# A two-layer gating and pooling encoder on one core: where ScalarE's roundings and norm steps stand in its queue

## The chip, the core and the metric

The kernel runs on one core of a Trainium2 chip. Its engines run side by side, each through its own queue in order: TensorE (PE) multiplies, VectorE (DVE) adds and subtracts, ScalarE (ACT) computes functions and copies, GpSimd (POOL) does little here, and SyncE (SP) issues the transfers from and to memory. The metric is the device time of one launch in microseconds. All times are in microseconds unless ns is written.

## The reference

Two groups of rows share the weights: 1024 rows of a prompt and 32 rows of a running stream, 1024 channels each. There are two layers. Layer 0 mixes rows by spatial gating, layer 1 by trailing means over 2, 4, 8 and 16 rows. Each layer then has a feed-forward net (FFN) with 4096 hidden channels.

```
def sgu_mixer(h, w_in, g_v, w_s, b_s, w_out, T):
    z = jax.nn.gelu(h @ w_in)
    u, v = jnp.split(z, 2, axis=-1)
    v = rmsnorm(v, g_v)
    ...
    s = jnp.einsum('gij,bnjgd->bnigd', w, vr)
    ...
    return (u * s) @ w_out, v

for i in range(DEPTH):
    mod = jax.nn.silu(c) @ w_ada[i] + b_ada[i]
    sh1, sc1, gt1, sh2, sc2, gt2 = jnp.split(mod[:, None, :], N_MOD, axis=-1)
    h = rmsnorm(x, g_norm[i, 0]) * (1 + sc1) + sh1
    ...
    x = x + gt1 * rmsnorm(mix, g_norm[i, 1])
    h = rmsnorm(x, g_norm[i, 2]) * (1 + sc2) + sh2
    f = jnp.square(jax.nn.relu(h @ ffn_w_up[i])) @ ffn_w_down[i]
    x = x + gt2 * rmsnorm(f, g_norm[i, 3])
```

## The kernel before

**Numbers in two halves.** Every fp32 operand of a product is split into a rounded high half and the rest: wh and wl of a weight, hh and hl of an input, fh and fl (FFN) or ush and usl (gating) of a hidden value. A product is three matmuls, wh by high, wh by low, wl by high (`products`, L1134 to L1136). ACT makes the high half by a Copy that rounds; DVE subtracts to get the low half. So a hidden costs one ACT and one DVE step (`split`, L1453) and a 512 KB weight piece of 128x1024 costs one ACT step (`do_w`, L592) and one DVE step.

**Tiles and passes.** The rows lie in three tiles of 384, 384 and 288 columns. Gating works over groups of 256 of its 2048 channels, FFN over chunks of 512 hidden channels. In gating, `sgu_item.up` makes pu = weights by input and gelu gives u (L1600); wsT is the transpose of the group's spatial weights, DVE copies it and scales it into wr, psp = wr by v is the spatial product, s = psp times u, and po collects the down product from ush and usl. In FFN, `ffn_item` makes pf, relu, square and the split, and pg collects the down product. The results are added up in acc.

**Pairs.** Two gating passes and chunks 1 to 7 of each FFN handle the first two tiles at once in a scheme with fewer products (`pair_item`). Its products pfa, pfb and pfc take combinations of the two tiles' inputs and of weight quarters (A1, S31, S24, A22, made by `quads`: subtractions on DVE, roundings L546 and L564 on ACT). In one step `up(jp)` PE makes A1 into pfa, S31 into pfb, S24 into pfa, S24 into pfb, S31 into pfa, A1 into pfc, A22 into pfa. Between products ACT copies pfa and pfb out (a1, b1, a2, a3, `copy`, L1764) and DVE adds them to the hidden sums r12, r22 and r11. The last product A22 goes into pfa and so needs a3 to be out. Each r gets relu, square (L1742, L1743) and a split.

**Weights' stream.** All weight pieces and the conditioning weights form one list. `issue` starts a piece's transfer on SP when one of three raw slots is free. `stream_step` rounds the next piece; `need_w` takes steps until a weight is there, and `weave`, called between products, takes a step or two ahead of need. `weave` also draws steps of the norms and residuals (generators in `fillers`), each of which yields a number of microseconds until its next step. The program keeps an account of PE's and DVE's time while it writes the instructions; `landed` is the account's time at issue plus LANDING, 5 us. `stream_waits` holds a step back while the piece has not landed in the account, but only if `last_copy` is set and the piece is not among the next two needed.

**Order.** A scheduler orders each engine's queue. `behind_copy()` puts an ACT step behind the step in `last_copy`. In the kernel before that is the newest `copy` of an FFN pair chunk; it is unset elsewhere: in gating, in the single FFN chunks, in the third tile's chunks, and after a pair chunk's second `up`. The roundings at L546, L564 and L592 all stand in `behind_copy()`.

**Norms.** `Stat.square` gathers squares; `split_sum` (L958) splits their sum into two halves (sc by an Identity on ACT, sm on DVE); `finish` waits, multiplies the halves by ones (pn, L1005) and takes Abs_reciprocal_sqrt and Square on ACT (L1009, L1010). The names end in rs, r_0x or r_1x by norm and tile.

Of the kernel before, what the change touches and what calls it, by code (L numbers as in the profile page):

```python
# [11 lines left out]
AF = mybir.ActivationFunctionType  # L12
# [4 lines left out]
D = 1024  # L17
# [18 lines left out]
def tile_stream_encoder_step(  # L36
# [26 lines left out]
    act = nc.scalar.activation  # L63
# [6 lines left out]
    def tick(us):  # L70
        time["pe"] += us
        time["dve"] = max(time["dve"], time["pe"] - 4.0)
# [33 lines left out]
    def acc_tile(t):  # L106
# [19 lines left out]
        out=quad, in_=ident.rearrange("p (c m) -> p m c", m=32), op=ALU.add, axis=AX.X  # L126
# [4 lines left out]
    epsT = const.tile([P, 1], F32, name="eps")  # L131
# [12 lines left out]
    def ps_up(name):  # L144
        return psum.tile([P, 512], F32, tag="pu", bufs=2, name=name)

    def ps_dn(name):
        return psum.tile([P, 512], F32, tag="pd", bufs=3, name=name)

    def ps_ms(name):  # L150
        return psum.tile([P, 512], F32, tag="pm", bufs=3, name=name)

    def t_m(name):
        return work.tile([P, 384], F32, tag="m", bufs=3, name=name)

    def t_c(name):
        return work.tile([P, 384], F32, tag="c", bufs=3, name=name)

    def t_hid(kind, name, dtype=F32R):
        return work.tile([P, 384], dtype, tag="h" + kind, bufs=5, name=name)  # L160
# [321 lines left out]
    last_copy = [None]  # L482

    def behind_copy():
        return ExitStack() if last_copy[0] is None else tc.issue_after(last_copy[0])
# [341 lines left out]
    def need_w(key):  # L827
        state["used"] = max(state["used"], wpos[key])
        while key not in witem:
            assert stream_ready(), key  # L830
            stream_step()
        return witem[key]
# [8 lines left out]
    def w_finish(key):  # L841
        w_free(key)
# [35 lines left out]
    def weave(streams=1):  # L878
        if streams:
            n = 0  # L880
            run_deferred()
            while n < streams and stream_ready() and not stream_waits():
                turn = bool(subs) and stream[state["next"]][0] == "wide"
                stream_step()
                n += not turn
        while time["dve"] < time["pe"] - slack[0] and fillers:
            if not pull():
                break

    def finish(tag):  # L890
        while any(f[0] == tag for f in fillers):
            pull(True)
        time["pe"] = max(time["pe"], time["dve"] - 3.0)
# [26 lines left out]
    class Stat:  # L920
# [4 lines left out]
        def __init__(self, t, tag, split=True, small=False):  # L925
            self.t, self.tag, self.n, self.split, self.small = t, tag, ncol[t], split, small
            self.todo = []
# [27 lines left out]

        def split_sum(self, sq):
            a, b = (x[:, : self.n] for x in self.parts)
            act(out=a, in_=sq, func=AF.Identity, bias=epsT)  # L958
            stt(out=b, in0=sq, scalar=epsT, in1=a.bitcast(F32), op0=ALU.add, op1=ALU.subtract)

        def square(self, k, src=None):
# [37 lines left out]

        def finish(self, out):  # L1000
            n = self.n
            yield 3.0 if gating_now[0] else 1.2
            pn = ps_ms(f"pn_{self.tag}")
            for i, x in enumerate(self.parts):
                mm(pn[:, :n], onesr, x[:, :n], start=i == 0, stop=i == 1)  # L1005
            tick(0.4)
            q = t_m(f"q_{self.tag}")[:, :n]
            r = work.tile([P, 384], F32, tag="rr", bufs=2, name=f"r_{self.tag}")[:, :n]
            act(out=r, in_=pn[:, :n], func=AF.Abs_reciprocal_sqrt, scale=1.0 / D)  # L1009
            act(out=q, in_=r, func=AF.Square)  # L1010
            yield 2.5
            stt(out=q, in0=pn[:, :n], scalar=-0.5 / D, in1=q, op0=ALU.mult, op1=ALU.mult)
            stt(out=r, in0=q, scalar=1.5, in1=r, op0=ALU.add, op1=ALU.mult)
            out.append(r)
            yield False


    gating_now = [True]
# [110 lines left out]
    def products(ps, n, terms, of=None):  # L1129

        i0, last = (0, len(terms) - 1) if of is None else (of[0], of[1] - 1)
        tick(3 * len(terms) * (0.004 + n / 2265.0))
        for i, (wh, wl, rh, rl) in enumerate(terms, i0):
            mm(ps[:, :n], wh, rh, start=i == 0, stop=False)  # L1134
            mm(ps[:, :n], wh, rl, start=False, stop=False)  # L1135
            mm(ps[:, :n], wl, rh, start=False, stop=i == last)  # L1136
# [100 lines left out]
    with tc.manual_schedule():  # L1237
# [63 lines left out]
        ps = ps_ms("pv0_5")  # L1301
# [105 lines left out]
    for p, b in v_order:  # L1407
        ps = ps_dn(f"pv{p}_{b}")
# [40 lines left out]
    def flush():  # L1449
        while pending:  # L1450
            pending.pop(0)()

    def split(dst_hi, dst_lo, src, n):  # L1453
        act(out=dst_hi[:, :n], in_=src[:, :n], func=AF.Copy)  # L1454
        tt(out=dst_lo[:, :n], in0=src[:, :n], in1=dst_hi[:, :n].bitcast(F32), op=ALU.subtract)

    def accumulate(t, d, ps, first):
        n = ncol[t]
        if first:
            act(out=A(t, d), in_=ps[:, :n], func=AF.Copy)  # L1460
        else:
            tt(out=A(t, d), in0=A(t, d), in1=ps[:, :n], op=ALU.add)

    def up_terms(wkey, t):
        wh, wl = need_w(wkey)
        return [
            (wh[:, k * P : (k + 1) * P], wl[:, k * P : (k + 1) * P], hh[t][:, k, :], hl[t][:, k, :])
            for k in range(KB)
        ]
# [106 lines left out]
    def sgu_item(p, t, mix, after):  # L1576
        gs, tiles = mixes[p]
        last = t == tiles[-1]
        n = ncol[t]
        hid = []  # L1580

        def put(g, k, s):
            a, b = t_hid("h", f"ush{g}_{t}_{k}"), t_hid("l", f"usl{g}_{t}_{k}")
            split(a, b, s, n)
            hid.append((a, b))

        inputs, factors, spatial, gate = gating(t, mix, put)
        us = []

        def up(g, k):  # L1590
            if k == 0:
                inputs(g)
            ps = ps_up(f"pu{g}_{t}_{k}")
            products(ps, n, up_terms(("u", p, g, k), t))
            if k == 0:
                factors(g)
            if last:
                w_finish(("u", p, g, k))
            u = t_m(f"u{g}_{t}_{k}")
            act(out=u[:, :n], in_=ps[:, :n], func=AF.Gelu_apprx_tanh)  # L1600
            us.append(u)

        def down():
            for d in range(KB):
                ps = ps_dn(f"po{gs[0]}_{t}_{d}")
                terms = []
                for j, (a, b) in enumerate(hid):
                    wh, wl = need_w(("o", p, gs[j // 2], d // 4))
                    o = (j % 2) * 512 + (d % 4) * P
                    terms.append((wh[:, o : o + P], wl[:, o : o + P], a[:, :n], b[:, :n]))  # L1610
                products(ps, n, terms)
                accumulate(t, d, ps, gs[0] == (4 if t == 0 else 0))
                if d == 0 and after is not None:
                    st = Stat(t, f"rs_{t}")
                if after is not None:
                    st.square(d)
                if last and d % 4 == 3:
                    for g in gs:
                        w_finish(("o", p, g, d // 4))
                weave(d % 2)  # L1620
            if after is not None:
                after(st)

        for j in range(4):
            up(gs[j // 2], j % 2)
            if j % 2 == 1:
                gate(gs[j // 2], spatial(gs[j // 2]), us)
            weave(2 if len(tiles) == 1 else 1)
            if j == 0:
                flush()  # L1630
        pending.append(down)
# [80 lines left out]
    def pair_item(p, after, ends, gate=None):  # L1712
        l, c, tiles, _ = passes[p] if gate is None else ("u", p[1], PAIR, 1)
        n = ncol[0]
# [47 lines left out]
        def copy(ps, name):  # L1762
            x = t_c(name)
            i = act(out=x, in_=ps[:, :n], func=AF.Copy)  # L1764
            if gate is None:
                last_copy[0] = i.ins
            return x

        def add(a, b, name):
# [4 lines left out]
        def up(jp):  # L1774
# [10 lines left out]
            if jp == 0:  # L1785
                flush()
                finish("combos" if gate is None else "usums")
                if state["kept"]:
                    state["kept"] = 0
                    for i in range(2):  # L1790
                        x = w_tile(f"fu{i}", ("fu", i))
                        u_places.append((x[:, :n], x[:, n : 2 * n]))
            quad_product(pb, jp, ("S31", 512), 1, True)
            b1 = copy(pb, f"b1{name}")
            hook(2, jp)
            weave()
# [61 lines left out]
        if passes[p + 1][2] != PAIR:  # L1858
            slack[0] = 0.0
            finish(f"ffn{l}_{NT - 1}")  # L1860
            fillers.append(late_norm.pop())
# [521 lines left out]
```

## Time and profile before

| what | value |
|---|---|
| median of 3 runs | 2099.66 us (2099.4 to 2100.45) |
| profiled execution | 2097.82 us, span 2096.0 us |
| granted TensorE clock | 0.999 |
| memory read and written | 271.09 MB and 30.66 MB |
| ACT busy, DVE busy | 51%, 78% of the span |

A row of a stretch gives the busy time of each engine in it. A row of the timeline gives start, duration, engine, line, operation, output and inputs, and in brackets the idle time ahead of it and what ended that. The end of a matmul is modelled: consecutive matmuls overlap in the drawing. L80 is the line of the DVE helper, so DVE's steps are told apart by their tiles.

### The profile page before, as it was taken

The page shows a single profiled execution, that of the slowest core. Times are in us where ns is not written, and L with a number is a line of the kernel's source. Part 1 is how long each engine was busy: PE and PEld are TensorE (multiplying, and loading weights), DVE is VectorE, ACT ScalarE, POOL GpSimd, SP SyncE. Part 2 cuts the span into 40 slices and gives each one's busy share as a digit, 9 for nine tenths or more (in the row PEclk, how much of TensorE's full clock was granted, in tenths as well). Part 3 has the DMA queues.
Part 4 walks back from the last instruction along what each step waited for, and adds up shares of the span by engine and source line. Part 5 has one row for each costly group of instructions (what it writes and reads, how often), then busy time and mean ns, then how long its engine had stood idle before and what let it go on. Part 6 is the DMA issues. An engine that isn't in the chain of part 4 may idle for free.

```text
span 2096.0 us, 32878 instructions
## 1 busy us (share of the span) xinstructions
PE 2075.2 (99%) x12742; PEld 2004.8 (96%) x12742; DVE 1636.7 (78%) x2953; ACT 1060.3 (51%) x1902; POOL 22.3 (1%) x44
## 2 busy tenths in 40 slices
PE   8999999999999999999999999999999999999998
PEld 6878999999999999999999999999999999999998
DVE  6799786889789998888868989896867654569554
ACT  5633443454247643344446766675435443365555
POOL 0000000000000000000000000000000000001100
PEclk9999999999999999999999999999999999999999
DMA  8585534365444443343424667643223221148863
GB/s 296 164 264 181 185 109 131 116 208 181 139 128 138 131 136 111 121 131 111 131 83 141 206 195 240 192 142 98 91 76 113 84 81 59 53 125 230 204 178 93
DMA packets 410737, 303.91 MB, mean 145 GB/s; under 512 B 47022, under 2 KB 373974, under 8 KB 410580
## 3 DMA queue, kind: packets, MB, share of 16 engines
q1 hardware_dynamic: 409652, 300.52, 47.4%
q8 instruction: 100, 1.64, 0.3%
q0 software_dynamic: 896, 1.28, 0.2%
q14 instruction: 57, 0.47, 0.1%
q10 hardware_dynamic: 32, 0.01, 0.0%
HBM read 271.09 MB, written 30.66 MB: 144 GB/s over the span
## 4 chain that ended last, share of the span: by engine, by line
PE 88%; DVE 7%; DMA 2%; ACT 2%; issue 1%; SPq 0%; DVEq 0%; ACTq 0%
PE pg L1135 11%; PE pg L1134 11%; PE pg L1136 11%; PE pf L1134 4%; PE pf L1136 4%; PE pf L1135 4%; PE pfa L1758 3%; PE pfa L1760 3%; PE pfa L1759 3%; PE pv L1160 2%; PE pv L1162 2%; PE pv L1161 2%; PE po L1134 2%; PE po L1135 2%; PE po L1136 2%; PE pu L1134 2%
## 5 line engine op out<-in xcount | busy, mean ns | idle before, releaser
L1134 PE MATMUL pg<-fh,wh_dn 128*128 128x384 f32 (+1 forms) x960 | 311.4, 325 | 1.4 <-ACT fh L1454 1.0
L1135 PE MATMUL pg<-fl,wh_dn 128*128 128x384 f32 (+1 forms) x960 | 310.4, 323 | 0.1
L1136 PE MATMUL pg<-fh,wl_dn 128*128 128x384 f32 (+1 forms) x960 | 309.9, 323 | 0.0
L80 DVE TENSOR_TENSOR acc<-acc,pg 128x384 f32<-128x384 f32 (+1 forms) x272 | 143.8, 533 | 106.0 <-PE pg L1136 105.4
L80 DVE TENSOR_TENSOR wl_dn<-raw,wh_dn 128x1024 fp32r<-128x1024 f32 x136 | 166.0, 1221 | 71.2 <-ACT wh_dn L592 43.0
L80 DVE SCALAR_TENSOR_TENSOR aa<-raw,csil,aa 128x512 f32<-128x512 f32 (+1 forms) x364 | 208.4, 619 | 6.3 <-DMA raw<-in_w_ada_dram 5.8
L1134 PE MATMUL pf<-hh,wh_up 128*128 128x288 f32 (+1 forms) x632 | 192.3, 305 | 0.0
L1135 PE MATMUL pf<-hl,wh_up 128*128 128x288 f32 (+1 forms) x632 | 191.1, 302 | 0.0
L1136 PE MATMUL pf<-hh,wl_up 128*128 128x288 f32 (+1 forms) x632 | 190.8, 302 | 0.0
L1134 PEld LDWEIGHTS pg<-fh,wh_dn 128*128 128x128 f32 x960 | 180.1, 188 | 3.0 <-ACT fh L1454 1.6
L592 ACT ACTIVATE wh_dn<-raw 128x1024 fp32r<-128x1024 f32 x136 | 143.7, 1057 | 75.2 <-PE pf L1135 34.0
L1135 PEld LDWEIGHTS pg<-fl,wh_dn 128*128 128x128 f32 x960 | 180.2, 188 | 1.0 <-DVE fl L80 0.6
L1136 PEld LDWEIGHTS pg<-fh,wl_dn 128*128 128x128 f32 x960 | 180.2, 188 | 0.0
L592 ACT ACTIVATE wh_up<-raw 128x1024 fp32r<-128x1024 f32 x79 | 83.6, 1058 | 79.0 <-PE pg L1135 46.0
L1136 PEld LDWEIGHTS pf<-hh,wl_up 128*128 128x128 f32 x632 | 118.9, 188 | 0.3 <-DVE wl_up L80 0.3
L1135 PEld LDWEIGHTS pf<-hl,wh_up 128*128 128x128 f32 x632 | 118.6, 188 | 0.5
L1134 PEld LDWEIGHTS pf<-hh,wh_up 128*128 128x128 f32 x632 | 118.5, 187 | 0.6 <-ACT wh_up L592 0.2
L80 DVE TENSOR_TENSOR wl_up<-raw,wh_up 128x1024 fp32r<-128x1024 f32 x79 | 96.4, 1220 | 28.7 <-ACT wh_up L592 28.7
L1134 PE MATMUL pg<-fx,wh_dn 128*128 128x288 f32 (+1 forms) x352 | 109.4, 311 | 0.2 <-ACT fx L1454 0.2
L1764 ACT ACTIVATE a<-pfa 128x384 f32<-128x384 f32 x84 | 40.9, 487 | 133.6 <-PE pfa L1760 133.5
L1135 PE MATMUL pg<-fx,wh_dn 128*128 128x288 f32 (+1 forms) x352 | 108.3, 308 | 0.0
L1136 PE MATMUL pg<-fx,wl_dn 128*128 128x288 f32 (+1 forms) x352 | 108.0, 307 | 0.0
(825 smaller groups left out, 5675.4 us busy)
## 6 DMA issues: line engine op xcount, KB each, us to landing
raw<-in_ffn_w_up_dram SPq DMA_DIRECT2D x136, 512.0 KB, 4.0
raw<-in_ffn_w_down_dram SPq DMA_DIRECT2D x136, 512.0 KB, 4.1
raw<-in_w_ada_dram SPq DMA_DIRECT2D x90, 512.0 KB, 4.2
raw<-in_sgu_w_in_dram SPq DMA_DIRECT2D x48, 512.0 KB, 4.4
raw<-in_sgu_w_out_dram SPq DMA_DIRECT2D x32, 512.0 KB, 3.6
xd<-acc SPq DMA_DIRECT2D x8, 1536.0 KB, 8.4
xo_r<-xd SPq DMA_DIRECT2D x32, 384.0 KB, 4.5
vd<-vt SPq DMA_DIRECT2D x32, 256.0 KB, 3.8
```

Of the source, the lines that this page charges most:

```text
L80: return op(out, *args, **kw)
L592: act(out=wh, in_=r, func=AF.Copy)
L1134: mm(ps[:, :n], wh, rh, start=i == 0, stop=False)
L1135: mm(ps[:, :n], wh, rl, start=False, stop=False)
L1136: mm(ps[:, :n], wl, rh, start=False, stop=i == last)
L1160: mm(ps[:m, :], a_h, wh[:, o : o + 512], start=k == 0, stop=False)
L1161: mm(ps[:m, :], a_h, wl[:, o : o + 512], start=False, stop=False)
L1162: mm(ps[:m, :], a_l, wh[:, o : o + 512], start=False, stop=k == KB - 1)
L1758: mm(ps[:, :n], wh[:, o], rh, start=first and k == 0, stop=False, skip_group_check=True)
L1759: mm(ps[:, :n], wh[:, o], rl, start=False, stop=False, skip_group_check=True)
L1760: mm(ps[:, :n], wl[:, o], rh, start=False, stop=k == HK - 1, skip_group_check=True)
L1764: i = act(out=x, in_=ps[:, :n], func=AF.Copy)
```

## The change

The two ACT steps of `finish` and the ACT step of `split_sum` are put into `behind_copy()`. The first pause of `finish` is 5.0 in place of 3.0 during gating (1.2 elsewhere, as before). `last_copy` is now also set by the high half of every hidden (`split`), by the gelu of `sgu_item.up` and by the copies of the gating pairs. With it set, `stream_waits` also holds steps back in the account outside FFN pair chunks. No instruction is added or removed, and the operands stay the same.

```
         def split_sum(self, sq):
             a, b = (x[:, : self.n] for x in self.parts)
-            act(out=a, in_=sq, func=AF.Identity, bias=epsT)
+            with behind_copy():
+                act(out=a, in_=sq, func=AF.Identity, bias=epsT)
...
         def finish(self, out):
             n = self.n
-            yield 3.0 if gating_now[0] else 1.2
+            yield 5.0 if gating_now[0] else 1.2
...
-            act(out=r, in_=pn[:, :n], func=AF.Abs_reciprocal_sqrt, scale=1.0 / D)
-            act(out=q, in_=r, func=AF.Square)
+            with behind_copy():
+                act(out=r, in_=pn[:, :n], func=AF.Abs_reciprocal_sqrt, scale=1.0 / D)
+                act(out=q, in_=r, func=AF.Square)
...
     def split(dst_hi, dst_lo, src, n):
-        act(out=dst_hi[:, :n], in_=src[:, :n], func=AF.Copy)
+        i = act(out=dst_hi[:, :n], in_=src[:, :n], func=AF.Copy)
+        last_copy[0] = i.ins
...
             u = t_m(f"u{g}_{t}_{k}")
-            act(out=u[:, :n], in_=ps[:, :n], func=AF.Gelu_apprx_tanh)
+            i = act(out=u[:, :n], in_=ps[:, :n], func=AF.Gelu_apprx_tanh)
+            last_copy[0] = i.ins
...
             i = act(out=x, in_=ps[:, :n], func=AF.Copy)
-            if gate is None:
-                last_copy[0] = i.ins
+            last_copy[0] = i.ins
```

## The prediction

> **What bounds the kernel now.** I read the page's busy times and its chain of waits first, then the busy time by stretches, then PE's waits.
>
> ```profile
> span 2096.0 us, 32878 instructions
> ...
> PE 2075.2 (99%) x12742; PEld 2004.8 (96%) x12742; DVE 1636.7 (78%) x2953; ACT 1060.3 (51%) x1902; POOL 22.3 (1%) x44
> ...
> PE 88%; DVE 7%; DMA 2%; ACT 2%; issue 1%; SPq 0%; DVEq 0%; ACTq 0%
> ```
>
> TensorE (PE) is busy 99% of the span, and most of the chain that sets the end is its matmuls. The change alters no matmul and adds no instruction; it only reorders. So what it can give or take is idle time of PE, which is 2096.0 - 2075.2 = 20.8 us.
>
> ```profile
> 0.00:50.00 50.00, 41.61 (x293) 29.48 (x294) 32.53 (x104) 28.94 (x56) 2.88 (x10) 1.00 0.89 306
> 450.00:500.00 50.00, 48.19 (x346) 47.15 (x345) 44.04 (x83) 33.44 (x49) 0.62 (x2) 1.00 0.69 216
> 600.00:650.00 50.00, 48.96 (x326) 47.94 (x326) 43.23 (x80) 30.94 (x56) 0.00 (x0) 1.00 0.47 146
> 700.00:750.00 50.00, 49.03 (x279) 48.05 (x278) 49.32 (x88) 26.17 (x46) 0.00 (x0) 1.00 0.46 141
> 2050.00:2096.00 46.00, 38.83 (x299) 38.41 (x297) 20.32 (x33) 22.07 (x46) 2.09 (x2) 0.95 0.27 83
> ```
>
> The columns are the stretch, its length, and the busy time of PE, weight loads, DVE, ACT and POOL. The first 50 us hold 8.4 us of the idle time and the last 46 us 7.2 us. The change reaches neither: the first instruction that changes place stands some 220 us in, and the last chunks keep their order. That leaves 5.2 us in the middle, of which 3.8 us lie in three stretches.
>
> ```profile
> PE pg L1134 <- ACT fh L1454: 1.0, 1, 1.0
> PE pn_r_0x L1005 <- ACT sc_r_0x L958: 0.9, 1, 0.9
> PE po L1135 <- DVE usl L80: 0.8, 1, 0.8
> PE pfa L1758 <- ACT a L1764: 0.7, 2, 0.5
> PE ada L710 <- DVE part L696: 0.6, 2, 0.3
> ```
>
> These waits (total, number, longest) name the middle. A matmul is drawn 0.33 us long though its follower normally starts 0.17 us later (226.26 and 226.44 below), so each wait costs some 0.16 to 0.25 us more than its idle time. With that, 5.2 us of idle time in about a dozen places are some 8 us that perfect reordering could win. That is the ceiling of the gain.
>
> **The change, part by part: what it wins.** Three edits put the norm's ScalarE (ACT) steps and the weights' rounding behind the newest urgent ACT step (gelu, copy, or high half of a hidden).
>
> ```profile
> 450.03 1.06 ACT L592 ACTIVATE wh_u<-raw 128x1024 fp32r<-128x1024 f32 x1 [2.26 <-DMA raw<-in_sgu_w_in_dram]
> 473.31 0.61 ACT L958 ACTIVATE sc_r_0x<-sq_r_0x,eps 128x384 fp32r<-128x384 f32 x1 [0.92 <-DVE sq_r_0x L80]
> 643.70 0.45 PE L1005 MATMUL pn_r_1x<-sm_r_1x,ones 128*128 128x384 f32 x1
> 645.13 0.80 PE L1134 MATMUL pg<-fh,wh_dn 128*128 128x384 f32 x3 [0.99 <-ACT fh L1454]
> 644.18 0.49 ACT L1009 ACTIVATE r_r_1x<-pn_r_1x 128x384 f32<-128x384 f32 x1 [0.35 <-PE pn_r_1x L1005]
> 644.57 0.51 ACT L1454 ACTIVATE fh<-r 128x384 fp32r<-128x384 f32 x1
> ```
>
> At 450 us ACT stands 2.26 us at a rounding whose load has not landed, and the hidden's split queues behind it. In the changed order the splits stand ahead of that rounding. The wait for usl goes: 0.8 idle, 0.95 with the drawing. What is late next is an accumulation 5 us on, of 0.3 us, which goes too. At 473 us the norm's matmul waits for a chain of squares; its matmuls move some 3 us of PE work later behind two more output blocks, so 0.9 to 1.0 us is won. At 643.70 PE stops 1.43 - 0.17 = 1.26 us, because the norm's reciprocal root (0.49) is ahead of the fh copy and itself waits for PE. The changed order puts fh first and gives it 5 us of PE work in advance: 1.26 us, and 0.2 us at its neighbour. Sum: 0.95 + 0.3 + 1.0 + 1.46 = 3.7 us. Of the pair chunks' waits for copies and for DVE (pfa 0.7, part 0.6 above, and smaller ones; DVE is full at 700 to 750, 49.32 of 50) the order changes some and leaves some: I count 1.3 us of about 4. Gain 5.0 us; from 3.0 (pair chunks nothing, one named site refilled) to 8.
>
> The yield of 5.0 in place of 3.0, and the 5 us landing in the account, only shift where norm steps and loads are issued. In the changed order no weight load has less than 10 us of PE work (matmuls counted at their spacing) between its issue and its use, so I cost their 512 KB loads at nothing; the median load-to-use distance hides them. SP has 195 of its 738 transfers later; what is queued behind is other loads with the same cover.
>
> **What it loses.** (A) The first gating groups, where gelu now heads the queue.
>
> ```profile
> 219.64 2.94 ACT L592 ACTIVATE wh_u<-raw 128x1024 fp32r<-128x1024 f32 x3
> 226.26 0.34 PE L1136 MATMUL pu<-hh,wl_u 128*128 128x384 f32 x1
> 226.44 0.27 PE L1485 MATMUL wsT<-ident,wt 128*128 128x128 f32 x1
> 226.75 0.29 DVE L1486 COPY wt<-wsT 128x128 f32<-128x128 f32 x1 [1.72 <-PE wsT L1485]
> 226.96 1.22 DVE L80 TENSOR_TENSOR wl_o<-raw,wh_o 128x1024 fp32r<-128x1024 f32 x1
> 229.08 0.28 DVE L80 TENSOR_SCALAR wr<-wt,rv 128x128 f32<-128x128 f32 x1
> 229.72 0.49 ACT L1600 ACTIVATE u<-pu 128x384 f32<-128x384 f32 x1
> ```
>
> Before, ACT rounds three wh_u at 219.64, ahead of the gelu, while PE is still in earlier work. PE so has a second group of pu ready when the first ends at 226.44. In the changed order the second and third of these roundings stand behind the first gelu, which needs that first group's end. PE then has only two transposes and the spatial product psp, which needs DVE's wr. The chain from 226.44: wt copy starts 0.31 later, a second copy 0.21 after it, two clears and the first wr, near 1.3 to 1.8 us in all. Say 1.6 us of standstill. Then the second group's weights: gelu (226.9 to 227.4), rounding 1.06, and on DVE, behind wr and psp's first result, wl 1.22, to about 231.2. PE reaches it after psp and two matmuls near 229.9: 1.2 us. The next group repeats this with half a us. Loss 3.3 us, from 2 (DVE ahead of my order) to 4.5.
>
> (B) Half of one combined weight, S31, moves behind a copy that waits for PE:
>
> ```profile
> 1531.84 1.15 ACT L564 ACTIVATE wh_up_S<-raw 128x512 fp32r<-128x512 f32 x2 [3.98 <-PE pg L1135]
> 1533.72 0.33 PE L1760 MATMUL pfa<-hh,wl_up_A 128*128 128x384 f32 x1
> 1534.09 0.49 ACT L1764 ACTIVATE a<-pfa 128x384 f32<-128x384 f32 x1 [1.10 <-PE pfa L1760]
> ```
>
> Here both halves are rounded 2 us before use. Changed, the half that the next product reads first comes after the copy: 1534.09 + 0.45 + 0.62 = 1535.2, and PE wants it at 1533.9: 1.3 us, up to 2.0 with its low half on DVE. I take 1.7.
>
> (C) In every pair chunk the S31 roundings now follow the first fh copy, and so stand just ahead of the copy a3 that the product A22 waits for.
>
> ```profile
> 1823.99 1.15 ACT L564 ACTIVATE wh_up_S<-raw 128x512 fp32r<-128x512 f32 x2
> 1825.31 0.33 PE L1760 MATMUL pfb<-hh,wl_up_S 128*128 128x384 f32 x1
> 1826.19 0.55 DVE L80 TENSOR_TENSOR r<-a,pfb 128x384 f32<-128x384 f32 x1
> 1826.77 0.52 ACT L1742 ACTIVATE r<-r 128x384 f32<-128x384 f32 x1 [1.64 <-DVE r L80]
> 1827.32 0.53 ACT L1743 ACTIVATE r<-r 128x384 f32<-128x384 f32 x1
> 1827.76 0.49 ACT L1764 ACTIVATE a<-pfa 128x384 f32<-128x384 f32 x1
> 1829.64 0.33 PE L1758 MATMUL pfa<-combo_hh,wh_up_A 128*128 128x384 f32 x1
> ```
>
> Counted from pfb's last matmul (1825.31), a3 now ends at 2.94 and A22 starts at 4.33, a reserve of 1.4 us. Changed: the sum r starts on DVE at 0.5 (the low half that kept it back to 0.88 is gone), relu 1.07, square 1.63, fh 2.2, two roundings 2.6 to 3.7, a3 to 4.2. The reserve is 0.1 us. In most of the 13 such chunks (the first one of layer 0 keeps its order) that costs nothing; where DVE has one operation ahead (0.4 us) it costs 0.3. I take 0.8 us; below, 0; above, 0.4 in each of 13 chunks.
>
> (D) Shorter leads at the first chunk of each layer's second tile and the first of layer 1, about 0.3 us each at three places, 0.4 at two last pair chunks, and 0.4 scattered in the gating pairs: 2.1 us, from 0 to 3.
>
> Sum: -5.0 + 3.3 + 1.7 + 0.8 + 2.1 = +2.9 us, on the profiled execution of 2097.82 us (span 2096.0 and 1.8 around it): 2100.7. The median of the runs is 2099.66, 1.84 above that execution, so the forecast is 2099.66 + 2.9 = 2102.6 us, inside the 0.2% (4.2 us) that I count as no change, since single runs here differ by 1 us.
>
> **The rivals.** *No reserve in the pair chunks.* For it: the 0.1 us of (C), and DVE's load of 49.32 in 50 us. Against it: in the changed order DVE's sum r stands behind nothing late in most chunks. It decides from 0.3 us of delay in each chunk: 13 x 0.4 = 5.2 in place of 0.8, giving 2102.6 + 4.4 = 2107.0, slower.
>
> *The reordering wins outright.* If DVE runs ahead in (A) (2.0 in place of 3.3), (B) waits only for the high half (1.3), (C) is nothing, (D) 0.5 and the gain is 8: -4.2 us, 2095.5, faster. For it: the three large waits are plain queueing, and the drawn order of DVE may not bind. Against: 226.44 leaves PE with no other work.
>
> *The order hardly matters.* If each moved step still has cover, gains and losses both under 1 us: 2099.7. Against: the 1.26 us at 643.70 has one cause and it moves.
>
> *A clock drop.* If the standstills of (A) lower the granted clock, their end is slower.
>
> ```profile
> 2080.00:2096.00 16.00, 8.83 (x71) 8.51 (x69) 5.70 (x13) 4.76 (x12) 2.09 (x2) 0.87 0.21 75
> ```
>
> Here 7.2 us of idle in 16 went with a clock of 0.87, 0.13 x 16 = 2.1 us; so 2104.7. Against: the first 50 us kept 1.00 with 8.4 us idle, and (A) has 1.6 us at one time. [...]
>
> **How the numbers follow.** Forecast 0.50 (own range 2098.5 to 2104), no reserve 0.28, outright win 0.10, hardly matters 0.08, clock drop 0.04. The range 2097.0 to 2108.0 leaves out the outer part of the win and of the slower rival. The forecast's upper edge, the clock case and the rival with no reserve end beyond 2103.9: slower 0.39. The win gives faster 0.09. The rest, 0.52, is no change.
>
> **What would show it.** Right: PE's waits for fh (L1454), sc_r_0x and usl near 450 to 645 us gone; PE idle some 3 us more in 200 to 250 us, with waits of psp for wr and of pu for wl_u; a wait of pfb for wh_up_S near 1535; a copies ending within 0.2 us of A22. Wrong: no idle time at 226 us; loads named as releasers of PE or ACT; repeated waits of pfa for a in each chunk (the slower rival); or middle idle time under 3 us.

## The result, and the profile after

The changed kernel takes 2114.12 us (median of 5 runs, 2110.65 to 2116.68); the kernel before, on the same chip, 2100.29 us (5 runs, 2099.4 to 2102.03). The ratio is 1.007, interval 1.0058 to 1.0081: slower by 13.8 us, above the range of the prediction. The profiled execution took 2116.28 us, so its account is 2.2 us larger than the median's.

Page of the changed kernel: span, busy times, shares of the chain of waits.

```profile
span 2114.5 us, 32793 instructions
...
PE 2082.1 (98%) x12742; PEld 2006.8 (95%) x12742; DVE 1640.8 (78%) x2953; ACT 1065.0 (50%) x1902; POOL 22.3 (1%) x44
...
PE 82%; DVE 10%; ACT 3%; DMA 3%; issue 2%; SPq 0%; DVEq 0%; ACTq 0%
```

No engine has more instructions than before. PE's idle time is 2114.5 - 2082.1 = 32.4 us, 11.6 more, and DVE's share of the chain goes from 7% to 10% while ACT's goes from 2% to 3%: what was reordered is ACT, what is late is DVE. PE's busy time also grew, by 6.9 us: matmuls after a stop are drawn longer (0.44 us at 866.07 and 870.04 us, 0.34 us at 964.76 us), and two stretches, 18.2 to 21.6 us and 482.4 to 489.3 us, ran at a granted clock of 0.50. The stretches of the changed kernel (columns as before):

```profile
200.00:250.00 50.00, 48.33 (x258) 41.90 (x257) 34.87 (x95) 20.84 (x37) 0.00 (x0) 1.00 0.50 154
450.00:500.00 50.00, 47.03 (x332) 46.77 (x332) 40.79 (x76) 28.91 (x45) 0.63 (x2) 0.93 0.75 239
600.00:650.00 50.00, 50.00 (x343) 49.63 (x342) 41.27 (x79) 25.49 (x43) 0.00 (x0) 1.00 0.43 132
800.00:1000.00 200.00, 196.09 (x1131) 192.92 (x1130) 163.92 (x263) 79.86 (x139) 0.00 (x0) 1.00 0.38 115
```

The gain at 600 to 650 us has come: PE stands nowhere, where 1.0 us was idle. The predicted loss at 200 to 250 us has come too. But 450 to 500 us lost more than it won, at a clock of 0.93, and 800 to 1000 us has 3.9 us of idle time, nearly all of it in two pair chunks, where the prediction had tenths of a us in a chunk. The same 200 us in the kernel before:

```profile
800.00:1000.00 200.00, 200.00 (x1166) 199.26 (x1165) 167.00 (x270) 80.94 (x142) 0.00 (x0) 1.00 0.37 116
```

PE's waits in the changed kernel (total, number, longest) give the new releasers:

```profile
PE pg L1136 <- DVE acc L80: 3.9, 4, 1.6
PE psp L1534 <- DVE wr L80: 3.0, 1, 3.0
...
PE pfa L1762 <- ACT a L1768: 1.7, 2, 1.0
PE pg L1137 <- DVE fx L80: 1.5, 1, 1.5
...
PE pg L1137 <- DVE combo_R L80: 1.3, 1, 1.3
```

The waits for fh, for sc_r_0x and for usl that the prediction named are gone. Four of the five shown in their place are for DVE, 9.7 of 11.4 us.

**The largest group: additions that come late.** In a pair chunk's down phase PE fills one of three buffers of pg per output block, and DVE's addition to acc frees it: PE's waits of pg for acc are the 3.9 us above. One such chunk of the changed kernel (timeline; ACT, DVE and PE apart):

```profile
853.83 0.52 ACT L1456 ACTIVATE fh<-r 128x384 fp32r<-128x384 f32 x1
854.24 1.05 ACT L592 ACTIVATE wh_dn<-raw 128x1024 fp32r<-128x1024 f32 x1
...
860.99 1.04 ACT L592 ACTIVATE wh_dn<-raw 128x1024 fp32r<-128x1024 f32 x1
862.93 1.06 ACT L592 ACTIVATE wh_dn<-raw 128x1024 fp32r<-128x1024 f32 x1 [0.89 <-DMA raw<-in_ffn_w_down_dram]
...
856.33 1.22 DVE L80 TENSOR_TENSOR wl_dn<-raw,wh_dn 128x1024 fp32r<-128x1024 f32 x1
...
862.35 1.22 DVE L80 TENSOR_TENSOR wl_dn<-raw,wh_dn 128x1024 fp32r<-128x1024 f32 x1
863.48 2.07 DVE L80 SCALAR_TENSOR_TENSOR aa<-raw,csil,aa 128x512 f32<-128x512 f32 x3
865.47 0.55 DVE L80 TENSOR_TENSOR acc<-acc,pg 128x384 f32<-128x384 f32 x1
...
868.31 1.21 DVE L80 TENSOR_TENSOR wl_dn<-raw,wh_dn 128x1024 fp32r<-128x1024 f32 x1
...
866.07 0.44 PE L1136 MATMUL pg<-fh,wh_dn 128*128 128x384 f32 x1 [0.35 <-DVE acc L80]
870.04 0.44 PE L1136 MATMUL pg<-fh,wh_dn 128*128 128x384 f32 x1 [1.33 <-DVE acc L80]
```

The same three pieces of weight in the kernel before. PE's work stands 9.3 us earlier here (the last product with fx starts at 855.72, in the changed kernel at 865.03), so 9.3 is added to compare:

```profile
840.17 1.05 ACT L592 ACTIVATE wh_dn<-raw 128x1024 fp32r<-128x1024 f32 x1
845.11 1.07 ACT L592 ACTIVATE wh_dn<-raw 128x1024 fp32r<-128x1024 f32 x1 [0.20 <-DMA raw<-in_ffn_w_down_dram]
850.76 1.04 ACT L592 ACTIVATE wh_dn<-raw 128x1024 fp32r<-128x1024 f32 x1
...
841.75 1.23 DVE L80 TENSOR_TENSOR wl_dn<-raw,wh_dn 128x1024 fp32r<-128x1024 f32 x1 [1.30 <-ACT wh_dn L592]
...
847.56 1.22 DVE L80 TENSOR_TENSOR wl_dn<-raw,wh_dn 128x1024 fp32r<-128x1024 f32 x1
...
856.15 1.22 DVE L80 TENSOR_TENSOR wl_dn<-raw,wh_dn 128x1024 fp32r<-128x1024 f32 x1
```

The first rounding stood at 849.5 by that shift; now it stands at 854.24, right behind the high half fh. Its low half was DVE's at 851.1, where DVE had been idle for 1.30 us; now it comes at 856.33, 5.3 us later, among other work. The next pair moves from 854.4 and 856.9 to 860.99 and 862.35, into the time of the additions, where it and three conditioning sums (aa, 2.07 us) stand ahead of an addition to acc. The third rounding waits 0.89 us for a load, and its low half at 868.31 (865.5 before) stands right ahead of the next additions. PE's starts lose 0.52 us at 865.38 and 1.52 us at 868.52; the next chunk loses 0.75 and 1.76 us in the same way: 4.55 us.

### The profile page after: what moved, and what is told of

Same layout as the page of the kernel before. It is cut to its first block, busy times and chain, and to the rows that moved or that the text cites. A ratio compares the mean times of both kernels' runs of the same rounds, so it can differ in the third digit from the quotient of the medians.

```text
span 2114.5 us, 32793 instructions
## 1 busy us (share of the span) xinstructions
PE 2082.1 (98%) x12742; PEld 2006.8 (95%) x12742; DVE 1640.8 (78%) x2953; ACT 1065.0 (50%) x1902; POOL 22.3 (1%) x44
## 3 DMA queue, kind: packets, MB, share of 16 engines
q0 software_dynamic: 896, 1.28, 0.2%
## 4 chain that ended last, share of the span: by engine, by line
PE 82%; DVE 10%; ACT 3%; DMA 3%; issue 2%; SPq 0%; DVEq 0%; ACTq 0%
PE pg L1137 10%; PE pg L1136 10%; PE pg L1138 10%; PE pf L1136 3%; PE pf L1137 3%; PE pf L1138 3%; PE pfa L1762 3%; PE pfa L1764 3%; PE pfa L1763 3%; PE pv L1162 2%; PE pv L1164 2%; PE pv L1163 2%; PE pu L1136 2%; PE po L1136 2%; PE pu L1138 2%; PE pu L1137 2%
## 5 line engine op out<-in xcount | busy, mean ns | idle before, releaser
L80 DVE TENSOR_TENSOR fl<-r,fh 128x384 fp32r<-128x384 f32 (+1 forms) x120 | 63.3, 527 | 55.0 <-ACT fh L1456 54.3
```

Of the source, the lines that this page charges most:

```text
L80: return op(out, *args, **kw)
```

## The experiments

All are compared with the kernel before on the same chip. "Above" is the difference of the two medians; the changed kernel is 13.8 us above. Theory 1 blames the high halves in `last_copy`, theory 2 the norm steps, theory 3 the account's landing wait. Line numbers move by a few where an edit adds lines.

**The edits undone one at a time.**

u_split, from the changed kernel:

```
     def split(dst_hi, dst_lo, src, n):
-        i = act(out=dst_hi[:, :n], in_=src[:, :n], func=AF.Copy)
-        last_copy[0] = i.ins
+        act(out=dst_hi[:, :n], in_=src[:, :n], func=AF.Copy)
```

> The change without its edit of split: the high halves of hiddens no longer set last_copy; all other edits stay. Theory 1 (roundings held back behind the hiddens' high halves make the weights' low halves arrive late and in a clump on VectorE, ahead of the additions that PE waits for): PE's waits for acc, combo_R, fx, fl, a and wh_up_S between 700 and 1600 us, some 13 us of standstill in the changed kernel against 5 in the kernel before, go back to 6 or less; total 2105 to 2108. The stop of psp for wr at 480 us stays. Theory 2 (the norm's steps behind the copies are the cause): total stays at 2111 to 2116. Theory 3 (the landing wait in the account holds the stream back): also little, since gelu and the pair copies still set last_copy in gating; but in the single chunks and the third tile's chunks last_copy is then unset and the wait is off there, 2108 to 2112.

2104.23 us against 2100.44 us, ratio 1.0019 (1.0009 to 1.0028): 3.8 above. This one edit carries 10 of the 13.8 us. The stretch with the late additions, in this kernel:

```profile
800.00:1000.00 200.00, 200.00 (x1164) 198.74 (x1163) 166.98 (x270) 80.28 (x141) 0.00 (x0) 1.00 0.40 119
```

PE is full again, as before the change. The wait for fh is back as well (1.0 us), so that gain needs the same edit. What is left of the loss is a stop of 2.06 us near 480 us, one of 1.29 us for b at 702 us, and (A).

u_norm takes the two `with behind_copy():` of `split_sum` and `finish` out again.

```
-            with behind_copy():
-                act(out=a, in_=sq, func=AF.Identity, bias=epsT)
+            act(out=a, in_=sq, func=AF.Identity, bias=epsT)
...
-            with behind_copy():
-                act(out=r, in_=pn[:, :n], func=AF.Abs_reciprocal_sqrt, scale=1.0 / D)
-                act(out=q, in_=r, func=AF.Square)
+            act(out=r, in_=pn[:, :n], func=AF.Abs_reciprocal_sqrt, scale=1.0 / D)
+            act(out=q, in_=r, func=AF.Square)
```

> The change without behind_copy in split_sum and finish; all else stays. Theory 2: the stop of 3.1 us at 480 us, where psp waits for wr behind the norm's squares on VectorE, goes, and with it the drop of the granted clock (0.74 and 0.58 in two stretches of 5 us), so 5 to 6 us: 2108 to 2110, and the spread between runs shrinks; in return PE waits again for fh behind the norm's reciprocal root near 645 us (1.3 us). Theory 1: unchanged in the pair chunks, the stop at 480 stays, 2111 to 2116.

2114.68 us against 2100.44 us, 1.0072 (1.0057 to 1.0087): nothing is won back, and the stop near 480 us stays, 2.72 us long. Of the 1.26 us at 643 us, 0.64 come back. Theory 2 falls.

u_land gives the landing wait a flag of its own, set only by the copies of FFN pair chunks, as before.

```
-        if last_copy[0] is not None and not near and time["pe"] < landed.get(state["next"], 1e9):
+        if land_copy[0] is not None and not near and time["pe"] < landed.get(state["next"], 1e9):
...
             last_copy[0] = i.ins
+            if gate is None:
+                land_copy[0] = i.ins
```

> The change with the landing wait of stream_waits kept to the feed-forward pair chunks, as before (a flag of its own that only their copies set); all roundings and norm steps stay behind the newest urgent step. Theory 3: the stream runs ahead again, the roundings come earlier in program order, and most of the loss goes: 2101 to 2105. Theories 1 and 2: the queue order behind the copies is what counts, 2110 to 2116.

2116.34 us against 2100.44 us, 1.0075 (1.0058 to 1.0092): theory 3 falls.

u_gelu and u_pair take the marking away from the gelu, and from the copies of the gating pairs.

```
-            i = act(out=u[:, :n], in_=ps[:, :n], func=AF.Gelu_apprx_tanh)
-            last_copy[0] = i.ins
+            act(out=u[:, :n], in_=ps[:, :n], func=AF.Gelu_apprx_tanh)
```

> The change without its edit of sgu_item.up: gelu no longer sets last_copy (split and the gating pairs' copies do). All theories: the stops at 227 to 232 us (2.3 us of PE) shrink to under 1 us, as the first gating groups then have no last_copy until the first split. Theory 1 and 2: the rest stays, so 2109 to 2114.

2111.69 us, 1.0058 (1.0043 to 1.0073): 11.3 above. The stops of (A) at 227 us are gone but for 0.32 us at 238 us.

```
-            last_copy[0] = i.ins
+            if gate is None:
+                last_copy[0] = i.ins
```

> The change with the copies of the gating pairs not setting last_copy, as before; all else stays. If the gating pairs' roundings held back behind their copies set the stream late for the third tile's gating, the stops at 417 (0.9 us) and at 480 us (3.1 us and the clock's drop after it) go: 2108 to 2110. If those stops come from the later norm steps or from gelu and split, nothing changes beyond 0.9 us: 2112 to 2116.

2111.13 us against 2099.09 us, 1.0062 (1.0047 to 1.0077): 12.0 above. The stop at 480 us (2.37 us) and the one at 417 us (0.96 us, 0.89 in the changed kernel) stay.

u_yield puts the pause of `finish` back to 3.0.

```
-            yield 5.0 if gating_now[0] else 1.2
+            yield 3.0 if gating_now[0] else 1.2
```

> The change with the first pause of finish at 3.0 in gating, as before. If the longer pause puts the residual's and the squares' work on VectorE into the spatial products' time, the stop of psp for wr at 480 us goes with the drop of the clock: 2108 to 2110. Otherwise 2112 to 2116. Nothing after 650 us should change, since the pause differs only in gating.

2110.25 us against 2099.09 us, 1.0057 (1.0042 to 1.0072): 11.2 above. The stop at 480 us is gone, at the price of 1.08 us at 453 us and 0.52 us at 477 us, and the clock there stays at 1.00 (450 to 500 us). The late additions stay. Each of these last three alone is not clear of the changed kernel's own interval.

**Sufficient and necessary.** o_split is the kernel before with the `split` edit alone (the landing wait kept on a flag as in u_land). u_split_gelu_yield is the changed kernel with three edits undone: `split`, gelu and pause.

```
     def split(dst_hi, dst_lo, src, n):
-        act(out=dst_hi[:, :n], in_=src[:, :n], func=AF.Copy)
+        i = act(out=dst_hi[:, :n], in_=src[:, :n], func=AF.Copy)
+        last_copy[0] = i.ins
```

> The kernel before with one edit of the change alone: the high half of every hidden (split) sets last_copy for the roundings; gelu and the gating pairs' copies do not, the norm's steps are free, the pause is 3.0, the landing wait is where it was. If split's edit is enough for the loss: 2106 to 2110, with waits for acc near 865 to 1000, for combo_R near 730, for fx near 1225, for a and wh_up_S near 1520 to 1550, and no stop at 227 us. If it takes the other edits with it (the landing wait above all): under 2104.

2111.58 us against 2099.58 us, 1.0057 (1.0043 to 1.0071): 12.0 above, more than expected. Its profile has the waits for acc (3.9 us in four places), and besides these one that nobody had forecast: the norm's matmul waits for sc_r_0x at 474 us, and PE loses 2.72 us there, where the kernel before loses 1.03.

```
-        last_copy[0] = i.ins          (split)
-            last_copy[0] = i.ins      (gelu)
-            yield 5.0 if gating_now[0] else 1.2
+            yield 3.0 if gating_now[0] else 1.2
```

> The change without split's and gelu's edits and with the pause at 3.0: left are the norm's steps behind the newest copy, the gating pairs' copies and the landing wait. If the three edits taken out carry the whole loss: 2098 to 2102, with no stop at 227 and none over 1.5 us at 480. If the rest costs too: 2103 to 2106.

2100.08 us against 2099.58 us, 1.0004 (0.9995 to 1.0014). So the high halves alone make nearly the whole loss, and without them, the gelu and the pause, what remains of the change (norm steps, gating pairs, landing wait) costs nothing that can be measured. From u_split to here 3.3 us go. Undone alone, the gelu and the pause had given 2.5 and 2.6 us, each within the noise, so these shares do not simply add up.

**Where in the program.** place_only is the kernel before with the `split` edit only in FFN pair chunks; place_off_gelu_yield is the changed kernel without it in those chunks, and with gelu and pause undone.

```
-    def split(dst_hi, dst_lo, src, n):
+    def split(dst_hi, dst_lo, src, n, note=False):
...
+        if note:
+            last_copy[0] = i.ins
...
-            split(a, b, r, n)
+            split(a, b, r, n, gate is None)
```

> The kernel before with split's edit in the feed-forward pair chunks alone (the high halves made in place set last_copy there, nowhere else). If the order inside the pair chunks carries the loss: 2106 to 2109, with the waits for a and combo_R at 705 to 730, for acc at 865 to 1000, and for a and wh_up_S at 1517 and 1546 us, some 9 us, and none of the other places. If the single chunks and the third tile's chunks carry it: under 2102.

2108.34 us against 2098.94 us, 1.005 (1.0034 to 1.0065): 9.4 above, at a clock of 0.999 in all four runs. Its waits of PE:

```profile
PE pg L1135 <- DVE acc L80: 3.9, 4, 1.6
PE pfa L1761 <- ACT a L1767: 2.3, 3, 1.1
...
PE pg L1136 <- DVE combo_R L80: 1.1, 1, 1.1
PE pfb L1761 <- ACT wh_up_S L565: 1.1, 1, 1.1
```

The waits for acc, a, combo_R and wh_up_S of the changed kernel are all here, with nothing changed outside the pair chunks.

```
+    def split(dst_hi, dst_lo, src, n, note=True):
...
-            split(a, b, r, n)
+            split(a, b, r, n, gate is not None)
```

> The change without split's edit in the feed-forward pair chunks, without gelu's edit and with the pause at 3.0; split's edit stays in gating, in the single chunks and in the third tile's chunks, and the norm's steps stay behind the newest step. If the pair chunks carry the loss: 2097 to 2101, with no wait for fh near 645 us. If the other chunks carry it: 2103 to 2107, with waits for fx near 1225 and for fl or fh near 1395.

2100.35 us against 2098.94 us, 1.0007 (0.9998 to 1.0016): the counterpart holds. The wait for wh_up_S is gone and that of pg for acc down to 0.5 us; those for fx and fl stay (0.87 and 0.76 us, start to start), so these two come from high halves outside the pair chunks.

**Which roundings.** dn_early holds wh_dn only behind the pair chunks' copies, as before the change; quad_early does so for A1, S31, S24 and A22. All else is the changed kernel.

```
-            with behind_copy():
+            with behind_pair() if key[0] == "dn" else behind_copy():
                 act(out=wh, in_=r, func=AF.Copy)
```

> The change, but the down weights' roundings (wh_dn) stay behind the pair chunks' copies alone, as before, not behind the hiddens' high halves. Theory 1, told closer: the later roundings of wh_dn push their low halves wl_dn on VectorE from the up phase into the down phase, where acc's additions must free pg's banks. Then the waits of pg for acc near 865, 868, 994 and 997 us (4.6 us), for combo_R at 734 (1.5) and for fx at 1229 (1.6) go, while the waits for a at 711 and 1523 and for wh_up_S at 1551 (3.3 us) stay: 2105 to 2108. If instead the roundings of the up weights are to blame, 2111 to 2115.

2114.22 us against 2099.09 us, 1.0076 (1.0061 to 1.0091): 15.1 above, no better. Its waits:

```profile
PE pg L1140 <- ACT fh L1460: 1.6, 2, 1.3
PE pg L1140 <- ACT fx L1460: 1.3, 1, 1.3
...
PE pg L1140 <- DVE acc L80: 1.0, 2, 0.5
```

The total was expected at 2105 to 2108 and is not lower at all. With wh_dn early the wait for acc falls from 3.9 us in four places to 1.0 in two, as expected, but new waits make up for it. PE waits seven times for a copy a. At 1229 us an early rounding (1.05 us, from 1227.21) and two steps of the norm's squares (0.85 and 0.83 us) stand ahead of fx. At 1430 us fh is late for another reason: a step of the norm's squares, which itself waits 1.28 us for acc, stands ahead of it.

```
-        with behind_copy():
+        with behind_pair():
             act(out=wh, in_=r, func=AF.Copy)
```

> The other half: the pair scheme's up roundings (A1, S31, S24, A22) stay behind the pair chunks' copies alone, as before; the down weights stay behind the newest urgent step as in the change. Theory 1 as told for dn_early: the waits for a at 711 and 1523 us and for wh_up_S at 1551 (3.3 us in all) go, those for acc, combo_R and fx stay: 2110 to 2113.

2111.61 us against 2099.09 us, 1.0067 (1.0051 to 1.0084): 12.5 above. The total is where it was expected, but by luck: the waits for a and wh_up_S, which were to go, stay (1.9 and 1.1 us), while those for acc, which were to stay, shrink to 0.7 us in three places, and those for combo_R grow to 2.5 us. So the late additions need both groups of roundings held back; with either one early most of them go. In both kernels the delay moves on to other steps of the chunks.

**Is a gain to be had?** norms_alone is the kernel before with only the norm steps behind the newest gelu, copy or high half (a variable of its own, which moves no rounding); one_norm does so for the one norm whose step delayed fh at 643 us.

```
-            act(out=a, in_=sq, func=AF.Identity, bias=epsT)
+            with behind_newest():
+                act(out=a, in_=sq, func=AF.Identity, bias=epsT)
```

> The kernel before with the one part of the change that should win: the norm's ScalarE steps (split_sum, finish) stand behind the newest gelu, copy or high half, kept in a variable of its own; the roundings, the pause and the landing wait are as in the kernel before. If the wait of pg for fh near 645 us came only from the reciprocal root's place: it goes (1.3 to 1.5 us), nothing else moves much, 2097 to 2099, ratio 0.9985 to 0.9998. If the scheduler gives it back elsewhere: 2099 to 2102.

2102.73 us against 2099.58 us, 1.0015 (1.0006 to 1.0024): slower by 3.2. The stop for fh falls from 1.26 to 0.57 us, but new ones come: 0.68 at 444 us, 3.1 in three pieces at 474 to 477 us, 1.43 at 1218 us; and in its profile the clock is 0.50 for 3.41 us behind those pieces, and 0.997 in the mean.

```
-            act(out=a, in_=sq, func=AF.Identity, bias=epsT)
+            with behind_newest() if self.tag == "r1_0_1x" else ExitStack():
+                act(out=a, in_=sq, func=AF.Identity, bias=epsT)
```

> The kernel before with one norm alone changed: the ScalarE steps of the norm of the second tile between mixing and FFN (r_1x of layer 0, split_sum and finish) stand behind the newest gelu, copy or high half; every other norm, the roundings, the pause and the landing wait are as before. Its reciprocal root then stands behind the fh copy that PE waited 1.26 us for near 645 us. If that wait was the root's place alone: it goes, nothing else moves, and the time falls by 1.0 to 1.5 us, ratio 0.9993 to 0.9996. If the wait's start is bound by relu and square anyway, or if it turns up behind the next step: 0.9997 to 1.0005.

2099.14 us against 2101.05 us, 0.9992 (0.9983 to 1.0001). fh is now ahead of the norm's reciprocal root, and PE loses 0.57 us there in place of 1.26. The 0.7 us fits the sign, but the interval touches 1: a win is not shown.

## Why the prediction was wrong

**Right: the gains.** The stops at 451 (usl), 473 (sc_r_0x) and 643 us (fh) went as worked out. In u_split the wait for fh is back, and in u_norm half of it, so it was the new order that took it away.

**Right: (A), a little smaller.** PE and ACT of the changed kernel at 227 us:

```profile
227.46 0.38 PE L1488 MATMUL wsT<-ident,wt 128*128 128x128 f32 x2
229.13 1.58 PE L1534 MATMUL psp<-wr,vl 128*128 128x128 f32 x12 [1.28 <-ACT wh_u L592]
...
227.66 0.49 ACT L1603 ACTIVATE u<-pu 128x384 f32<-128x384 f32 x1 [1.87 <-PE pu L1138]
```

PE has two transposes and then psp, and the roundings stand behind the gelu at 227.66, as predicted. The stop is 1.45 us for the predicted 1.6; the ones behind it are 0.55 and 0.26 us for 1.2 and 0.5. Sum 2.3, inside its bounds of 2 to 4.5. (The row names wh_u, the releaser that came last by the profile; which of wh_u and wr holds psp here is not told apart.)

**Right: (B).** Rounding and product at the place forecast:

```profile
1551.86 0.49 ACT L1768 ACTIVATE a<-pfa 128x384 f32<-128x384 f32 x1 [1.26 <-PE pfa L1764]
1552.25 0.62 ACT L564 ACTIVATE wh_up_S<-raw 128x512 fp32r<-128x512 f32 x1
...
1552.92 0.44 PE L1762 MATMUL pfb<-hh,wh_up_S 128*128 128x384 f32 x1 [1.10 <-ACT wh_up_S L564]
```

1.26 us lost, against 1.7 taken and 1.3 as the lower bound: PE waits for the high half only.

**Right in kind, low in size: (C), and with it the rival of no reserve falls.** One pair chunk:

```profile
967.34 1.14 ACT L564 ACTIVATE wh_up_S<-raw 128x512 fp32r<-128x512 f32 x2
968.38 0.47 ACT L1768 ACTIVATE a<-pfa 128x384 f32<-128x384 f32 x1
...
964.76 0.34 PE L1764 MATMUL pfb<-hh,wl_up_S 128*128 128x384 f32 x1
...
969.09 0.34 PE L1762 MATMUL pfa<-combo_hh,wh_up_A 128*128 128x384 f32 x1
```

From pfb's last matmul, a3 starts at 3.62 and ends at 4.09, A22 starts at 4.33; the prediction had 3.7, 4.2 and 4.33. In most chunks it costs nothing. Where DVE was late with r12, PE stood: 0.86 us at 711 us and 1.20 us at 1523 us. That is 2.06 us for the 0.8 taken; the first of the two places had cost 0.71 us in the kernel before. But it is not 0.4 us in each of 13 chunks.

**Smaller than costed at its own places: (D).** (D) stands with 2.1 us. Of the places that it names, two have a new late start above 0.3 us: 0.78 us for fl at 1398 us, in the first chunk of layer 1, and 0.9 us for acc at 417 us, in a gating pair. Three other late starts lie where (D) had nothing. At 1229 us, in the third tile's chunks of layer 0, 1.62 us are lost for fx, with two steps of the residual and the norm (0.96 and 0.95 us) ahead of it on DVE. At 1048 us 0.35 us are lost for part, which the kernel before has too (0.38). And 2.06 us go in three starts of combo_R's products from 730 to 736 us, in the down phase of layer 0's first pair chunk. There a low half wl_dn (1.22 and 1.21 us on DVE, from 729.00 and 734.58) stands right ahead of both combo_R steps, so this is the trouble of the late additions again. Fl, fx, part and combo_R together are 4.8 us.

**The step that failed** is the count of the pair chunks, which ends with (C): that "DVE's sum r stands behind nothing late in most chunks" was true, and it was taken for all of DVE. The prediction followed the up phase and its roundings. It didn't follow the roundings of the down weights, held back behind the same high halves, to DVE: each has a low half of 1.2 us, which used to come earlier, in part in DVE's idle time, and now came, in queue order, just ahead of additions that free pg's buffers. That is 4.55 us for acc, which the prediction put at nothing. With combo_R (2.06), a (2.06) and wh_up_S (1.26) the late starts of the pair chunks are 9.9 us, where the prediction had 0.8 for (C) and 1.7 for (B). The 9.4 us of place_only, against the 10 that u_split wins back, show that the pair chunks carry the loss. That the held wh_dn cause the late additions is read from the queues; dn_early supports it, but quad_early shows that the held up roundings have a part in it.

The rounding that waited 0.89 us for its load is a sign that the prediction had named against itself: not all loads were covered. Such waits of wh_dn are not new, but they grew from 12.1 us in 8 places to 18.8 in 13.

**A second step failed: the pause costed at nothing.** At 480 us, in the changed kernel, on DVE and PE:

```profile
478.87 0.95 DVE L80 TENSOR_TENSOR sq_r_0x<-sq_r_0x 128x768 f32<-128x768 f32 x1
479.73 1.22 DVE L80 TENSOR_TENSOR ring<-raw,ring 128x1024 fp32r<-128x1024 f32 x1
480.87 1.21 DVE L80 TENSOR_TENSOR wl_u<-raw,wh_u 128x1024 fp32r<-128x1024 f32 x1
...
482.77 0.62 DVE L80 TENSOR_SCALAR wr<-wt,rv 128x128 f32<-128x128 f32 x3
...
479.87 0.27 PE L1488 MATMUL wsT<-ident,wt 128*128 128x128 f32 x1
```

After the transpose at 479.87 PE has nothing but psp, which needs wr. Ahead of wr stand steps of the norm's squares (0.95 and, before wr, 0.56 us) and two low halves. From start to start PE loses 3.13 us. With the pause back at 3.0 (u_yield) this stop is gone, with the norm steps undone (u_norm) it stays. It is the mechanism of (A), PE with only psp left, at a place where the prediction counted a gain. The pause is not the only way to lose there: in o_split, with the pause at 3.0, PE lost 2.72 us at 474 us for sc_r_0x.

**The sum.** Start by start, PE lost 2.3 (A), 0.9 (pgu for acc at 417 us), 3.1 (480 us), 2.1 (a, two places), 4.8 (combo_R, fx, fl and part), 4.55 (acc) and 1.3 (B): 19.0 us. With the 5.0 us of gains that the prediction counted taken off, 14.0 remain. As a check, all starts between 200 and 2100 us that are more than 0.2 us late add up to 11.3 us in the trace before and 24.8 us in the one after: 13.5 us more.

The profiled execution is 18.5 us slower than that of before (2116.28 - 2097.82), which leaves 4.5 us. Of these 1.0 us is no effect of the change: up to 219 us both kernels do the same work in the same order, and the same matmul starts at 208.44 us before and at 209.46 us after. In that part the clock was 0.50 from 18.21 to 21.62 us in the changed kernel's execution and 1.00 in that of before. Some 2.4 us go to the lower clock behind the stop at 480 us: from 473 to 507 us the same work falls back by another 4.5 us, of which the stop explains 3.1, while 1.0 is won at sc_r_0x. The last 1.1 us are a remainder and not measured by themselves.

**The clock rival** had a lower clock behind a standstill, and one was measured, but in another place: the clock stayed at 1.00 in (A)'s stretch (225 to 235 us, longest stop 1.45 us) and fell to 0.50 behind the stop of 3.13 us at 480 us. What was held against it, that the first 50 us kept 1.00 with 8.4 us idle, does not hold for every execution: in the changed kernel's profile the same first part has the 0.50 named above.

## What to carry to other kernels

A rounding that is moved on ACT drags a step of DVE with it (here 1.22 us behind 1.05), and a load behind that; a move on one engine is costed by following its outputs through the queues of all the others, up to what frees the buffers that PE writes. Holding all background work behind the newest urgent step turns even work into a lump after it: here few urgent steps had been late before, and the lump fell on the additions. Where an engine is at 98 to 99%, a rule for all steps can cost more than all the stops that it is meant for, as here: 13.8 us, where the prediction put those stops at some 8. To take one stop away with the step that causes it (one_norm) did no harm, but that it wins is not shown.

## What the hardware showed that was not expected

Behind a single stop of 3.13 us the granted clock fell to 0.50, and of two stops of 2.72 us one was followed by 0.50 and one by 1.00. In the changed kernel's profile the moments at which the granted clock changes lie a whole number of stretches of 3.41 us apart: it is 0.50 from 18.21 to 21.62 us, one such stretch; it falls again at 482.42 us, 135 stretches later, is back at 489.25 us, two later, and falls once more at 2110.58 us, 475 later. Rows of stretches of that length of the changed kernel, of u_gelu and of u_norm, two rows each (PE's busy time first, the granted clock behind the busy times):

```profile
479.01:482.42 3.41, 1.13 (x9) 0.87 (x7) 3.31 (x5) 2.23 (x3) 0.00 (x0) 1.00 1.07 393
482.42:485.83 3.41, 2.72 (x13) 2.72 (x13) 2.48 (x8) 0.61 (x1) 0.00 (x0) 0.50 1.04 336
...
479.26:482.68 3.42, 1.81 (x15) 1.82 (x16) 3.33 (x9) 0.87 (x2) 0.18 (x1) 1.00 1.03 342
482.68:486.09 3.41, 3.41 (x12) 3.41 (x11) 3.25 (x12) 1.98 (x4) 0.13 (x1) 0.50 0.95 325
...
481.82:485.23 3.41, 1.94 (x15) 1.94 (x16) 3.01 (x10) 0.99 (x2) 0.30 (x1) 1.00 1.05 350
485.23:488.65 3.42, 3.42 (x22) 3.42 (x21) 3.42 (x11) 0.93 (x3) 0.01 (x1) 1.00 1.05 342
```

In the changed kernel the stop of 3.13 us leaves PE 2.28 us idle within one stretch of 3.41 us, and the clock is 0.50 for the next two, up to 489.25 us: 3.4 us of clock are missing, some of them while PE stood. The matmuls of 384 columns start 0.32 us apart at the lower clock (from 486.15 us) and 0.17 us apart behind it (from 489.31 us). In u_gelu and u_norm the stop has the same length, 2.72 us from start to start. In u_gelu 1.61 us of it fall into one stretch, and the clock is 0.50 for the next. In u_norm the cut at 481.82 us divides it into 1.08 and 1.47 us, and the clock stays at 1.00.

The traces of the two kernels, cut into such stretches behind their first 7 us, show this. Ahead of a fall to 0.50 PE is idle for 1.63 us (14.80 to 18.21 us), 2.28 us (479.01 to 482.42) and 3.14 us (2107.16 to 2110.57) in the changed kernel, and for 2.75 us (2088.30 to 2091.71) in the kernel before. The most idle time in a stretch at 1.00 with 1.00 behind it is 1.35 us (868.13 to 871.54) in the changed kernel and 1.07 us (9.58 to 13.00) in the kernel before. In the first 7 us it is otherwise: in the changed kernel PE has no matmul from 1.14 to 4.55 us, and the clock behind is 1.00. This sorts two traces; no run moved a stop on purpose.

In the five runs of the changed kernel a lower mean clock and a longer time go together: 2110.65 us at a mean clock of 0.999, 2113.9 and 2114.12 at 0.998, 2116.28 and 2116.68 at 0.997. Not all of it belongs to the change: the clock's fall at 18.21 us in the changed kernel's profile is ahead of everything that the change moves, and in the profile of the kernel before the clock is 1.00 there.
